# Stick-breaking attention scores on Trainium2: stacking the high and low parts of a head over 128 rows

## The chip, the cores and the metric

The kernel runs on one core of one Trainium2 chip. The metric is the time of the kernel in device microseconds (us). The profile gives one execution in detail: five engines work side by side on their own instruction streams, TensorE (PE, whose weight loads PEld run beside its products), VectorE (DVE), ScalarE (ACT), GpSimd (POOL) and SyncE (SP, which issues most transfers). PSUM, where products are accumulated, has eight banks of 128 partitions by 512 float32 columns.

## The reference

One decoder layer over 512 tokens of width 1024, in three sub-layers: a SwiGLU feed-forward block (inner width 2816), a mixing block, and a second feed-forward block. Each is modulated by vectors computed from a condition, gated, added to the residual and normalised. The mixing block runs two branches side by side. The one that matters here is attention with 16 heads of 64:

```python
z = jnp.einsum('bhqd,bhkd->bhqk', qb, kb).astype(jnp.float32) * scale
mask = s_idx < t_idx
log_keep = jnp.where(mask, jax.nn.log_sigmoid(-z), 0.0)
between = lax.cumsum(log_keep, axis=3, reverse=True) - log_keep
log_w = jax.nn.log_sigmoid(z) + between
w = jnp.where(mask, jnp.exp(log_w), 0.0)
outs.append(jnp.einsum('bhqk,bhkd->bhqd', w.astype(vb.dtype), vb))
```

A weight is thus the sigmoid of its score times the product of (1 - sigmoid) of all later scores in the row. The other branch is a gated linear unit (glu), a causal depthwise convolution of width 31, a normalisation and a swish.

## The kernel before

**Precision.** A product of two float32 matrices is made from parts: each operand is split into a high part, rounded to the matmul format F32R, and a low part, the rest. High times high, high times low and low times high are accumulated in one PSUM bank, so a float32 product takes three matmuls. For a result that is itself an operand of the next product (q, k, v, the attention weights), ACT copies the bank into the high part, and DVE subtracts the high part from the bank into the low part.

**Before the attention.** The first feed-forward block ends with the normalisation of each 128-token tile and its transposition into u2, the input of the mixing block. `dense_group` (L378) then makes the projections of the first pair of heads (q, k, and glu's two halves), four tiles of 128 output channels by 512 tokens, and `run(v_tasks(0))` the first group of v.

**The unit loop (L733).** Attention goes by units. A unit `i` is one head and one tile of 128 query tokens: pair of heads j = i // 8, head hh in the pair, token tile tb, 64 units in all. A tile of q or k holds one pair, head 0 in partitions 0 to 63, head 1 in 64 to 127. An iteration of the loop does, in this order:

- `att_scores(i)` (L623): the scores z of the unit, 128 queries by n = (tb + 1) x 128 keys, from three matmuls whose contraction runs over the 64 rows of the head (L630 to L632). Two sigmoids on ACT (L635, L636) give nb = sigmoid(-z) and be = sigmoid(z), a scan on DVE (L637) the running product of nb, and POOL masks and multiplies (L640, L642).
- `advance`: one or two half tasks from a list `tasks` made beforehand: a projection tile is two halves of 12 matmuls, a group of v (two pairs of heads) four blocks of 24. A planner orders them by due times: q and k of pair j are due two units before the pair begins, and a group of v at the start of the pairs that use it. The other tasks, glu and gates, fill the rest. Weights are fetched three tasks ahead (`AHEAD`).
- `att_values(i - 3)` (L661): weights times v, three matmuls for each of the tb + 1 key tiles into 64 columns (128*64 tiles) of the bank po.
- `att_transpose(i - 2)` (L645): the weights are transposed by PE (pw, L652) and split into wTh (ACT, L655) and wTl (DVE, L656).
- `bg`: on average 3.8 (`CONV_PACE`) pieces of background work, the taps of the depthwise convolution on DVE (L527). A finished glu pair adds 32 pieces to the list.
- in each fourth of the first 32 iterations, one multiplication or addition on POOL over a residual tile (L316).

**Buffers that the change touches.** Projections and v pass through three PSUM banks (tag `ps`). The first half of a glu pair keeps its bank until the second half is evicted (`glu_done`, L566). Scores have two banks (`z`). The parts of q and k (`qh`, `ql`, `kh`, `kl`) have two buffers each, so that pair j + 1 can be written while pair j is read. The parts of v (`vh`, `vl`) are tiles of 4 x 256 columns, one for a group of two pairs, two buffers each. The buffers of a tag are handed on: a new tile is written only after the last reader of the tile that had its place. Waits between engines are worked out from such reads and writes. The order on each engine is made when the program is built; it follows the order of the text, where what an instruction needs is there.

**After the attention** come five rounds of a gate tile and a tile of the attention's output projection, with 14 background pieces each (L830), the normalisation of the convolution, which needs all taps, and the rest of the merge.

Of the kernel before, what the change touches and what calls it, by code (L numbers as in the profile page):

```python
# [7 lines left out]
F32 = mybir.dt.float32  # L8
F32R = mybir.dt.float32r
# [5 lines left out]
P = 128  # L15
S = 512
D = 1024
KC = D // P
NT = S // P
# [3 lines left out]
DH = 64  # L23
# [20 lines left out]
def decoder_block(ctx: ExitStack, tc: tile.TileContext, a: dict, out: bass.AP):  # L44
    nc = tc.nc
# [463 lines left out]
    at_cm, ap_ = open_pool("mixa", "left")  # L509
# [3 lines left out]
    qk = {}  # L513
    vq = {}
# [16 lines left out]
            background.append(lambda i=i: tap(i))  # L531
        background.append(lambda: nc.vector.tensor_add(acc, acc, accs[1]))

    def parts_of(ps, name, bufs):
        hi = ap_.tile([P, S], F32R, tag=name + "h", name=name + "h", bufs=bufs)
        lo = ap_.tile([P, S], F32R, tag=name + "l", name=name + "l", bufs=bufs)
        nc.scalar.copy(hi, ps)
        nc.vector.tensor_sub(lo, ps, hi.bitcast(F32))
        return hi, lo

    def gate_tile(name):
        return gp.tile([P, S], F32, tag="g", name=name, bufs=4)

# [8 lines left out]
    def tile_tasks(src, name, done):  # L552
        st = {}
        return [(lambda: st.update(w=load_added(src)), lambda: half_dense(st, name, 0, done)),
                (None, lambda: half_dense(st, name, 1, done))]

    def set_qk(j, x, ps):
        qk[j, x] = parts_of(ps, x, 2)

    def qk_tasks(j):  # L560
        out_ = []
# [28 lines left out]
    def v_tasks(q):  # L590
        st = {}

        def block(t):
            if t == 0:
                st["h"] = ap_.tile([P, NT, 256], F32R, tag="vh", name="vh", bufs=2)
                st["l"] = ap_.tile([P, NT, 256], F32R, tag="vl", name="vl", bufs=2)
                vq[q] = (st["h"], st["l"])
            if t % 2 == 0:
                st["ps"] = bank("psv")
            ps = st["ps"]  # L600
            o = ps[:, (t % 2) * 256 : (t % 2) * 256 + 256]
            tsl = slice(t * P, (t + 1) * P)
            for k in range(KC):
                wh, wl = st["w"][k // 4]
                cs = slice((k % 4) * 256, (k % 4) * 256 + 256)
                nc.tensor.matmul(o, u2[0][:, k, tsl], wh[:, cs], start=(k == 0), stop=False)
                nc.tensor.matmul(o, u2[0][:, k, tsl], wl[:, cs], start=False, stop=False)
                nc.tensor.matmul(o, u2[1][:, k, tsl], wh[:, cs], start=False, stop=(k == KC - 1))
            if t % 2 == 1:
                dst = st["h"][:, t - 1 : t + 1, :]  # L610
                pv = ps.rearrange("p (t e) -> p t e", t=2)
                nc.scalar.copy(dst, pv)
                nc.vector.tensor_sub(st["l"][:, t - 1 : t + 1, :], pv, dst.bitcast(F32))

        def fetch():
            st["w"] = [load_added(a["w_v"][q, h]) for h in range(2)]

        return [(fetch if t == 0 else None, lambda t=t: block(t)) for t in range(NT)]
# [3 lines left out]

    def att_scores(i):  # L623
        j, hh, tb = i // 8, (i // 4) % 2, i % 4
        (qh, ql), (kh, kl) = qk[j, "q"], qk[j, "k"]
        rs = slice(hh * DH, (hh + 1) * DH)
        n = (tb + 1) * P
        tsl = slice(tb * P, (tb + 1) * P)
        z = bank("z", "z")
        nc.tensor.matmul(z[:, :n], qh[rs, tsl], kh[rs, :n], start=True, stop=False)  # L630
        nc.tensor.matmul(z[:, :n], qh[rs, tsl], kl[rs, :n], start=False, stop=False)
        nc.tensor.matmul(z[:, :n], ql[rs, tsl], kh[rs, :n], start=False, stop=True)  # L632
        nb = ap_.tile([P, S], F32, tag="nb", name="nb", bufs=2)
        be = ap_.tile([P, S], F32, tag="be", name="be", bufs=LAG + 1)
        nc.scalar.activation(nb[:, :n], z[:, :n], AF.Sigmoid, scale=-QSCALE)  # L635
# [24 lines left out]

    def att_values(i):  # L661
        j, hh, tb = i // 8, (i // 4) % 2, i % 4
        vh, vl = vq[j // 2]
        wh, wl = unit.pop(i)
        rs = slice(hh * DH, (hh + 1) * DH)
        vs = slice((j % 2) * P + hh * DH, (j % 2) * P + (hh + 1) * DH)
        tsl = slice(tb * P, (tb + 1) * P)
        if tb == 0:
            heads["po"] = bank("po", "po")
# [320 lines left out]
```

## Time and profile before

| | |
|---|---|
| Time, median of 3 runs | 1331.72 us (1330.6 to 1331.79) |
| The profiled execution: its own time | 1331.39 us |
| Its span (first to last instruction) | 1329.7 us |
| Granted TensorE clock, mean | 0.995 |
| PE busy / PEld busy | 1289.2 us (97%) / 1068.7 us |
| DVE / ACT / POOL busy | 739.4 / 523.0 / 567.8 us |
| Unit loop, first score product to the start of the last gate tile in it | 422.8 to 729.2 us |
| Score products in it | 192, first start 422.8, last 712.0 us |

The times come from runs without a profile; every duration comes from the one profiled execution. Matmuls overlap in their pipeline, so the duration of one says less than the distance from its start to the next start. A wait "x <- y" is idle time of the engine just before x that ended when y did. A line such as L630 is the line of the kernel that issued the instruction; in helpers such as `dense` (L144 to L146) the tile's name tells which projection it is.

### The profile page before, as it was taken

To read this page: it belongs to the slowest core of one execution; us is meant where nothing else is said; L and a number is where in the kernel's file an instruction comes from. 1 tells how busy PE (TensorE), PEld (TensorE's weight loads), DVE (VectorE), ACT (ScalarE), POOL (GpSimd) and SP (SyncE) were. 2 spreads that over 40 slices of the span, in tenths; PEclk is the share of its full clock that TensorE was granted. 3 is DMA by queue.
4 is the path that set the end of the run, shared out by engine and by line. 5 is a ranking of instruction groups with operands and counts; after the bars stand their busy time and mean duration, and the time that the engine had idled before them with its cause. 6 is when DMAs were issued, how large, how long until landed. Compare 5 with 4: busy or idle time off the path is not lost.

```text
span 1329.7 us, 16789 instructions
## 1 busy us (share of the span) xinstructions
PE 1289.2 (97%) x6444; PEld 1068.7 (80%) x6444; DVE 739.4 (56%) x1017; ACT 523.0 (39%) x793; POOL 567.8 (43%) x392
## 2 busy tenths in 40 slices
PE   5899999999999999999999999997999999999997
PEld 4688888888889878878778888885898888888886
DVE  7886920255463959498788865366682000025545
ACT  2233322222256555555555648422452222222220
POOL 3464544644312564533443111142254566564434
PEclk9999999999999999999999999998999999999999
DMA  9668843232328474656466985974283333323321
GB/s 358 216 213 310 299 160 94 97 96 95 95 83 196 103 174 96 140 129 130 110 144 132 237 196 112 294 219 140 68 281 96 96 110 97 114 101 93 102 65 63
DMA packets 57856, 197.88 MB, mean 149 GB/s; under 512 B 6688, under 2 KB 6832, under 8 KB 57776
## 3 DMA queue, kind: packets, MB, share of 16 engines
q1 hardware_dynamic: 47952, 161.15, 36.6%
q0 software_dynamic: 9824, 35.66, 15.7%
q8 instruction: 50, 0.82, 0.2%
q14 instruction: 30, 0.25, 0.1%
HBM read 194.70 MB, written 2.10 MB: 148 GB/s over the span
## 4 chain that ended last, share of the span: by engine, by line
PE 85%; DVE 10%; DMA 2%; ACT 1%; POOL 1%; issue 1%; SPq 0%; DVEq 0%; POOLq 0%; ACTq 0%
PE y L357 19%; DVE ada L189 3%; DVE cacc L527 2%; PE z L630 1%; PE q L144 1%; PE glub L144 1%; PE glua L144 1%; PE pw L652 1%; PE ga L146 1%; PE ga L144 1%; PE ga L145 1%; PE gb L146 1%; PE gb L145 1%; PE gb L144 1%; PE q L145 1%; PE glub L145 1%
## 5 line engine op out<-in xcount | busy, mean ns | idle before, releaser
L114 POOL TENSOR_TENSOR wlo<-raw,whi 128x1024 fp32r<-128x1024 f32 x88 | 223.3, 2543 | 244.4 <-ACT whi L113 240.2
L113 ACT CAST whi<-raw 128x1024 fp32r<-128x1024 f32 x144 | 149.6, 1046 | 275.2 <-issue 50.6
L137 POOL TENSOR_TENSOR raw<-raw,mod_g 128x1024 f32<-128x1024 f32 x52 | 131.4, 2532 | 154.8 <-DMA raw<-in_dn 85.8
L527 DVE SCALAR_TENSOR_TENSOR cacc<-h,cv_w,cacc 128x512 f32<-128x512 f32 x232 | 173.8, 809 | 0.0
L130 ACT CAST whi<-raw 128x1024 fp32r<-128x1024 f32 x68 | 71.3, 1049 | 123.7 <-PE ga L145 19.9
L114 DVE TENSOR_TENSOR wlo<-raw,whi 128x1024 fp32r<-128x1024 f32 x56 | 104.7, 1871 | 23.6 <-ACT whi L113 23.6
L357 PE MATMUL y<-whi,sh 128*128 128x512 f32 x352 | 113.7, 390 | 0.0
L357 PE MATMUL y<-wlo,sh 128*128 128x512 f32 x352 | 113.6, 389 | 0.0
L357 PE MATMUL y<-whi,sl 128*128 128x512 f32 x352 | 113.6, 389 | 0.0
L189 DVE SCALAR_TENSOR_TENSOR ada<-ada,crow 128x512 f32<-128x512 f32 x96 | 92.0, 1007 | 13.5 <-DMA ada<-in_ada_t 8.3
L642 POOL TENSOR_TENSOR be<-be,nb 128x127 f32<-128x127 f32 (+1 forms) x64 | 55.0, 860 | 102.8 <-DVE nb L637 101.4
L422 DVE TENSOR_TENSOR sl<-sF,sh 128x512 fp32r<-128x512 f32 x44 | 45.3, 1031 | 85.4 <-ACT sh L421 85.4
L421 ACT CAST sh<-sF 128x512 fp32r<-128x512 f32 x44 | 27.1, 623 | 143.7 <-PE y L357 132.0
L132 POOL DMA_DIRECT2D wlo<-in_w_in x44 | 38.4, 873 | 92.2 <-ACT wlo L131 88.4
L357 PEld LDWEIGHTS y<-whi,sl 128*128 128x128 f32 x352 | 66.1, 188 | 13.7
L357 PEld LDWEIGHTS y<-wlo,sh 128*128 128x128 f32 x352 | 66.1, 188 | 13.7
L357 PEld LDWEIGHTS y<-whi,sh 128*128 128x128 f32 x352 | 66.1, 188 | 13.6
L131 ACT ACTIVATE wlo<-whi 128x1024 fp32r<-128x1024 f32 x68 | 72.1, 1061 | 0.9
L637 DVE TENSOR_TENSOR_SCAN nb<-nb,future 128x127 f32<-128x127 f32 (+1 forms) x64 | 60.3, 942 | 2.0 <-ACT nb L635 1.8
L640 POOL TENSOR_SCALAR_AFFINE_SELECT be<-be 128x128 f32<-128x128 f32 x64 | 43.4, 678 | 22.6 <-ACT be L636 22.0
L224 DVE SCALAR_TENSOR_TENSOR acc<-ada,silu_c,acc 128x1024 f32<-128x1024 f32 x21 | 43.6, 2078 | 14.4 <-DMA ada<-in_ada_w 14.2
L656 DVE TENSOR_TENSOR wTl<-pw,wTh 128x128 fp32r<-128x128 f32 (+1 forms) x64 | 30.5, 477 | 32.2 <-ACT wTh L655 32.1
(496 smaller groups left out, 3362.4 us busy)
## 6 DMA issues: line engine op xcount, KB each, us to landing
raw<-in_gu SPq DMA_DIRECT2D x80, 512.0 KB, 3.6
raw<-in_w_in SPq DMA_DIRECT2D x48, 512.0 KB, 3.6
raw<-in_dn SPq DMA_DIRECT2D x44, 512.0 KB, 3.5
wlo<-in_w_in POOLq DMA_DIRECT2D x44, 512.0 KB, 6.9
ada<-in_ada_t SPq DMA_DIRECT2D x32, 512.0 KB, 5.1
ada<-in_ada_w SPq DMA_DIRECT2D x24, 512.0 KB, 4.8
ada<-in_ada SPq DMA_DIRECT2D x32, 256.0 KB, 6.0
raw<-in_gu_first SPq DMA_DIRECT2D x8, 512.0 KB, 6.4
```

The lines of the kernel that those rows point to most:

```text
L113: nc.scalar.copy(hi, raw)
L114: lo_eng.tensor_sub(lo, raw, hi.bitcast(F32))
L130: nc.scalar.copy(hi, raw)
L131: nc.scalar.mul(lo, hi.bitcast(F32), -1.0)
L137: nc.gpsimd.tensor_mul(raw, raw, G)
L144: nc.tensor.matmul(ps[:, c0:c1], wh[:, ks], mov(uh, k)[:, c0:c1], start=(k == 0), stop=False)
L145: nc.tensor.matmul(ps[:, c0:c1], wh[:, ks], mov(ul, k)[:, c0:c1], start=False, stop=False)
L189: ins = nc.vector.scalar_tensor_tensor(raw[:, qs], raw[:, qs], 1.0, crow[:, qs], ALU.mult, ALU.mult, accum_out=parts[:, q : q + 1])
L357: nc.tensor.matmul(acc[t][h][:, c0 - h * 512 : c1 - h * 512], st[:, tsl], wt[:, c0:c1], start=(k == 0 and i == 0 and c0 % 512 == 0), stop= ...
L527: ins = nc.vector.scalar_tensor_tensor(o, hv, cv_w[:, j, i : i + 1], o, ALU.mult, ALU.add)
L637: nc.vector.tensor_tensor_scan(nb[:, 1:n][:, ::-1], nb[:, 1:n][:, ::-1], future[:, S - n + 1 : S][:, ::-1], 1.0, ALU.mult, ALU.max)
L642: nc.gpsimd.tensor_mul(be[:, 0 : n - 1], be[:, 0 : n - 1], nb[:, 1:n])
```

## The change

- `att_scores` makes z from two matmuls instead of three, each with a contraction over all 128 partitions. For head hh, `q1` holds the high part of the head's q twice (in the head's own 64 partitions and in the other 64), `k12` the high part of k in the own partitions and the low part in the others, so their product is hi x hi + hi x lo. `q2` holds the low part of q in the own partitions and zeros in the others; its product with `k12` is lo x hi.
- `set_qk` builds these tiles per head. For q, two ACT copies of 64 partitions (own, then other) and one DVE subtraction per head; for k, one ACT copy and one DVE subtraction per head, the subtraction written into the other partitions. The tiles `q0`, `q1`, `k0`, `k1` have two buffers each. The `q2` tiles are four that stay (`qlow`, by parity of j and by head).
- Before the first dense group, the zero halves of the four `qlow` tiles are written: one memset on POOL, four ACT copies of 64 partitions.
- The parts of v are kept by pair of heads, tiles of 4 x 128 columns with three buffers each instead of tiles for two pairs with two buffers. At the first block of a group both pairs' tiles are allocated, and each eviction of a bank (after the second and the fourth block) is two ACT copies and two DVE subtractions of 256 columns instead of one each of 512.

```diff
--- before.py
+++ after.py
@@ -531,13 +531,6 @@
             background.append(lambda i=i: tap(i))
         background.append(lambda: nc.vector.tensor_add(acc, acc, accs[1]))
 
-    def parts_of(ps, name, bufs):
-        hi = ap_.tile([P, S], F32R, tag=name + "h", name=name + "h", bufs=bufs)
-        lo = ap_.tile([P, S], F32R, tag=name + "l", name=name + "l", bufs=bufs)
-        nc.scalar.copy(hi, ps)
-        nc.vector.tensor_sub(lo, ps, hi.bitcast(F32))
-        return hi, lo
-
     def gate_tile(name):
         return gp.tile([P, S], F32, tag="g", name=name, bufs=4)
 
@@ -554,8 +547,32 @@
         return [(lambda: st.update(w=load_added(src)), lambda: half_dense(st, name, 0, done)),
                 (None, lambda: half_dense(st, name, 1, done))]
 
+
+
+    half = [slice(0, DH), slice(DH, P)]
+    qlow = [[ap_.tile([P, S], F32R, **({} if i + hh else {"align_bytes": 256}), name=f"ql{i}{hh}") for hh in range(2)]
+            for i in range(2)]
+    zero = ap_.tile([P, S], F32, tag="nb", name="zero", bufs=2)
+    nc.gpsimd.memset(zero, 0.0)
+    for set_ in qlow:
+        for hh in range(2):
+            nc.scalar.copy(set_[hh][half[1 - hh], :], zero[half[1 - hh], :])
+
     def set_qk(j, x, ps):
-        qk[j, x] = parts_of(ps, x, 2)
+        both = []
+        for hh in range(2):
+            own, other = half[hh], half[1 - hh]
+            t = ap_.tile([P, S], F32R, tag=f"{x}{hh}", name=f"{x}{hh}", bufs=2)
+            nc.scalar.copy(t[own, :], ps[own, :])
+            if x == "q":
+                low = qlow[j % 2][hh]
+                nc.vector.tensor_sub(low[own, :], ps[own, :], t[own, :].bitcast(F32))
+                nc.scalar.copy(t[other, :], ps[own, :])
+                both.append((t, low))
+            else:
+                nc.vector.tensor_sub(t[other, :], ps[own, :], t[own, :].bitcast(F32))
+                both.append(t)
+        qk[j, x] = both
 
     def qk_tasks(j):
         out_ = []
@@ -592,9 +609,8 @@
 
         def block(t):
             if t == 0:
-                st["h"] = ap_.tile([P, NT, 256], F32R, tag="vh", name="vh", bufs=2)
-                st["l"] = ap_.tile([P, NT, 256], F32R, tag="vl", name="vl", bufs=2)
-                vq[q] = (st["h"], st["l"])
+                for j in (2 * q, 2 * q + 1):
+                    vq[j] = [ap_.tile([P, NT, P], F32R, tag="v" + x, name="v" + x, bufs=3) for x in "hl"]
             if t % 2 == 0:
                 st["ps"] = bank("psv")
             ps = st["ps"]
@@ -607,10 +623,12 @@
                 nc.tensor.matmul(o, u2[0][:, k, tsl], wl[:, cs], start=False, stop=False)
                 nc.tensor.matmul(o, u2[1][:, k, tsl], wh[:, cs], start=False, stop=(k == KC - 1))
             if t % 2 == 1:
-                dst = st["h"][:, t - 1 : t + 1, :]
                 pv = ps.rearrange("p (t e) -> p t e", t=2)
-                nc.scalar.copy(dst, pv)
-                nc.vector.tensor_sub(st["l"][:, t - 1 : t + 1, :], pv, dst.bitcast(F32))
+                for j in range(2):
+                    h_, l_ = vq[2 * q + j]
+                    dst, part = h_[:, t - 1 : t + 1, :], pv[:, :, j * P : (j + 1) * P]
+                    nc.scalar.copy(dst, part)
+                    nc.vector.tensor_sub(l_[:, t - 1 : t + 1, :], part, dst.bitcast(F32))
 
         def fetch():
             st["w"] = [load_added(a["w_v"][q, h]) for h in range(2)]
@@ -622,14 +640,12 @@
 
     def att_scores(i):
         j, hh, tb = i // 8, (i // 4) % 2, i % 4
-        (qh, ql), (kh, kl) = qk[j, "q"], qk[j, "k"]
-        rs = slice(hh * DH, (hh + 1) * DH)
+        (q1, q2), k12 = qk[j, "q"][hh], qk[j, "k"][hh]
         n = (tb + 1) * P
         tsl = slice(tb * P, (tb + 1) * P)
         z = bank("z", "z")
-        nc.tensor.matmul(z[:, :n], qh[rs, tsl], kh[rs, :n], start=True, stop=False)
-        nc.tensor.matmul(z[:, :n], qh[rs, tsl], kl[rs, :n], start=False, stop=False)
-        nc.tensor.matmul(z[:, :n], ql[rs, tsl], kh[rs, :n], start=False, stop=True)
+        nc.tensor.matmul(z[:, :n], q1[:, tsl], k12[:, :n], start=True, stop=False)
+        nc.tensor.matmul(z[:, :n], q2[:, tsl], k12[:, :n], start=False, stop=True)
         nb = ap_.tile([P, S], F32, tag="nb", name="nb", bufs=2)
         be = ap_.tile([P, S], F32, tag="be", name="be", bufs=LAG + 1)
         nc.scalar.activation(nb[:, :n], z[:, :n], AF.Sigmoid, scale=-QSCALE)
@@ -660,10 +676,10 @@
 
     def att_values(i):
         j, hh, tb = i // 8, (i // 4) % 2, i % 4
-        vh, vl = vq[j // 2]
+        vh, vl = vq[j]
         wh, wl = unit.pop(i)
         rs = slice(hh * DH, (hh + 1) * DH)
-        vs = slice((j % 2) * P + hh * DH, (j % 2) * P + (hh + 1) * DH)
+        vs = rs
         tsl = slice(tb * P, (tb + 1) * P)
         if tb == 0:
             heads["po"] = bank("po", "po")
```

## The prediction

> **What bounds the kernel now.** I read the page first: the engine totals, then the chain of work that ended last.
>
> ```profile
> PE 1289.2 (97%) x6444; PEld 1068.7 (80%) x6444; DVE 739.4 (56%) x1017; ACT 523.0 (39%) x793; POOL 567.8 (43%) x392
> PE 85%; DVE 10%; DMA 2%; ACT 1%; POOL 1%; issue 1%; SPq 0%; DVEq 0%; POOLq 0%; ACTq 0%
> ```
>
> PE carries the span, so time taken from PE's stream shortens it, as long as nobody else is late there. DVE's 56% is a mean over stages, and the change lies in one: the unit loop, from the first score product to the last gate tile in it (the attention stage). I cut it into seven stretches of iterations of the unit loop. The list of background convolution taps, at 3.8 an iteration, has work in the first, third, fifth and seventh stretch (iterations 0-8, 14-22, 29-44, 48-66) and runs dry in the others (9-13, 23-28, 45-47); this follows from when the loop finishes each glu pair. The view of busy time by stretch:
>
> ```profile
> 422.76:461.21 38.45, 37.09 (x228) 30.11 (x227) 33.70 (x46) 19.73 (x38) 20.11 (x23) 1.00 0.65 140
> 461.21:486.86 25.65, 25.22 (x154) 20.26 (x153) 12.70 (x18) 15.16 (x27) 16.75 (x18) 1.00 0.63 144
> 486.86:526.34 39.48, 39.48 (x242) 31.66 (x241) 36.11 (x51) 21.91 (x43) 18.92 (x25) 1.00 0.63 134
> 526.34:556.59 30.25, 29.09 (x193) 24.41 (x193) 16.96 (x19) 16.04 (x30) 18.94 (x17) 1.00 0.45 105
> 556.59:630.05 73.46, 73.08 (x461) 59.68 (x461) 62.12 (x94) 41.76 (x79) 31.12 (x45) 1.00 0.61 137
> 630.05:643.28 13.23, 13.23 (x77) 10.37 (x77) 11.60 (x18) 7.76 (x15) 6.31 (x10) 1.00 0.60 126
> 643.28:729.16 85.88, 85.88 (x496) 68.58 (x496) 73.69 (x113) 45.63 (x83) 33.34 (x47) 1.00 0.60 128
> ```
>
> Columns: stretch, its length, then busy time of PE, PEld, DVE, ACT and POOL, granted clock, DMA share, GB/s. PE is busy 303 of 306 us. DVE is the runner-up: 85 to 91% in the four tap stretches. The clock is 1.00 throughout.
>
> **What a unit costs on PE.** One unit in order of time, the values of an older unit first; then the weight loads of the first score product and of the next dense product:
>
> ```profile
> 559.76 0.39 PE L146 MATMUL glub<-uh,wlo 128*128 128x512 f32 x1
> 559.98 0.22 PE L675 MATMUL po<-wTh,vh 128*64 128x128 f32 x1
> ...
> 560.46 0.22 PE L677 MATMUL po<-wTh,vl 128*64 128x128 f32 x1
> 560.52 0.62 PE L652 MATMUL pw<-ident,be 128*128 128x128 f32 x4
> 561.07 0.44 PE L630 MATMUL z<-kh,qh 64*128 64x384 f32 x1
> 561.35 0.34 PE L631 MATMUL z<-kl,qh 64*128 64x384 f32 x1
> 561.53 0.33 PE L632 MATMUL z<-kh,ql 64*128 64x384 f32 x1
> 561.79 0.50 PE L144 MATMUL glua<-uh,whi 128*128 128x512 f32 x1
> 562.13 0.40 PE L145 MATMUL glua<-ul,whi 128*128 128x512 f32 x1
> 562.36 0.40 PE L146 MATMUL glua<-uh,wlo 128*128 128x512 f32 x1
> ```
>
> ```profile
> 561.07 0.18 PEld L630 LDWEIGHTS z<-kh,qh 64*128 64x128 f32 x1 [0.17 <-issue]
> 561.79 0.19 PEld L144 LDWEIGHTS glua<-uh,whi 128*128 128x128 f32 x1 [0.25 <-issue]
> ```
>
> Durations overlap, so what counts is start to start. In the dense stream a 512-column product takes 0.23 us (562.13 to 562.36), its weights loaded ahead. The step from dense into the values tile (559.76 to 559.98) is no longer than that. But at both edges of the 64-row score products the weight load stands idle 0.17 and 0.25 us and starts only together with its own product. For comparison, transposes followed by a dense product where all tiles are 128*128:
>
> ```profile
> 803.72 1.04 PE L799 MATMUL ptb<-ident,cn 128*128 128x128 f32 x8
> 804.52 0.48 PE L144 MATMUL ysb<-ph,whi 128*128 128x512 f32 x1
> 804.83 0.40 PE L145 MATMUL ysb<-pl,whi 128*128 128x512 f32 x1
> ```
>
> Eight transposes and one product take 1.11 us: less 0.23, that is 0.11 a transpose and nothing over. In the unit, four transposes and the first score product take 561.35 - 560.52 = 0.83, where 4 x 0.11 + 0.18 = 0.62 would do: 0.21 over. From the last score product to the second dense one are 562.13 - 561.53 = 0.60, where 0.18 + 0.23 = 0.41 would do: 0.19 over. So each unit pays about 0.40 us for entering and leaving the 64-row shape.
>
> **What the change takes off PE.** Two score products replace three; the steps that they take, from the rows (384 columns: 0.18 above):
>
> ```profile
> 552.58 0.27 PE L631 MATMUL z<-kl,qh 64*128 64x128 f32 x1
> 552.69 0.27 PE L632 MATMUL z<-kh,ql 64*128 64x128 f32 x1
> 556.81 0.28 PE L631 MATMUL z<-kl,qh 64*128 64x256 f32 x1
> 556.93 0.27 PE L632 MATMUL z<-kh,ql 64*128 64x256 f32 x1
> 565.94 0.39 PE L631 MATMUL z<-kl,qh 64*128 64x512 f32 x1
> 566.17 0.39 PE L632 MATMUL z<-kh,ql 64*128 64x512 f32 x1
> ```
>
> That is 0.11, 0.12, 0.18 and 0.23 us, 0.64 for four units, 16 x 0.64 = 10.2 us in all. Contracting 128 rows instead of 64 costs nothing per product: 0.23 for 512 columns at either height. The scores now have the 128*128 shape of their neighbours, so the 0.40 goes too, 64 x 0.40 = 25.6. Gross 35.8 us, 0.56 a unit. Bounds for the edge: 0 (it was something else, and stays) and 0.40; I take all of it, since the row of 128*128 neighbours shows no excess.
>
> One rule speaks against the last step. The Trainium skill, TensorEngine Tiling, Key Properties, says that changing the tiling mode drains the TensorE. By that rule the change of shape at the values tile (128*64) drains as well, and if the 0.40 is shared by all four changes of a unit, the sum loses half of it, 12.8 us. The trace agrees at the 64-row edges (0.17 and 0.25 idle) and shows no drain at the 64-column tile (0.22 from dense to values).
>
> **What it adds.** Rows for evictions, scan and weighting:
>
> ```profile
> L679 ACT COPY yF<-po 64x512 f32<-64x512 f32 x16 | 9.2, 577 | 20.5 <-PE po L677 20.4
> L538 DVE TENSOR_TENSOR ql<-q,qh 128x512 fp32r<-128x512 f32 x7 | 4.8, 688 | 9.9 <-ACT qh L537 9.7
> L656 DVE TENSOR_TENSOR wTl<-pw,wTh 128x256 fp32r<-128x256 f32 x16 | 6.5, 406 | 2.3 <-ACT wTh L655 2.3
> L637 DVE TENSOR_TENSOR_SCAN nb<-nb,future 128x511 f32<-128x511 f32 x16 | 21.5, 1342 | 0.9 <-ACT nb L635 0.9
> L642 POOL TENSOR_TENSOR be<-be,nb 128x511 f32<-128x511 f32 x16 | 17.5, 1092 | 26.9 <-DVE nb L637 26.5
> ```
>
> ACT takes 0.58 us for 64x512, and moves it to other partitions for the second head, so half the partitions is not half the time. Each q tile now takes four ACT copies for one and two DVE subtractions for one; each k tile two and two. In the stage (seven pairs) that is 7 x 4 x 0.58 = 16 us on ACT, whose busy time is 168 of 306: hidden by its idle time. On DVE it is 14 x 0.69 = 9.6 us, if a subtraction on 64 partitions takes as long as one on 128. Splitting six v evictions adds 6 x (2 x 0.41 - 0.69) = 0.8.
>
> This is where the gain is cut. Per stretch I take off 0.56 x units (9, 5, 9, 6, 16, 3, 16) from the length, add to DVE 1.4 for each pair of q and k and 0.13 for each v eviction, and let the later end count: 33.4 against 35.2 (DVE); 22.9 against 14.2 (PE); 34.4 against 37.5 (DVE); 26.9 against 18.6 (PE); 64.5 against 65.2 (DVE); 11.6 against 11.6; 76.9 against 75.1 (PE). The sum of the later ones is 276.2, so 306.4 - 276.2 = 30.2 is left of 35.8; DVE takes 5.6. A backlog of one iteration would be made up in the dry stretches: at best this loss is 0.
>
> Three smaller terms. The evictions, first. The PSUM bank of a projection is freed by the subtraction, and in two places PE waits for that now (the view of waits, then the chain at one of them):
>
> ```profile
> PEld k L144 <- DVE ql L538: 1.6, 2, 0.8
> ```
>
> ```profile
> 547.69 0.59 ACT qh L537
> 548.31 0.70 DVE ql L538
> 549.05 0.50 PE k L144
> ```
>
> There glu's two banks are held, and the rest passes through the third. The eviction takes 0.59 + 0.70 = 1.3 us; with four copies, the second subtraction ends some 1.0 later. Two places: 2.0 us (bounds 0 and seven times 1.0).
>
> The v tiles, second. Before there were two buffers of two pairs; now there are three of one pair, filled two at a time. The second pair's buffer is free only when the pair three back has had its last values: iteration 10 for the group evicted at 7, iteration 26 for the one evicted at 23, and the bank stays held meanwhile. Around 23 only one bank is free (glu again), so v, q and k stand behind it, and PE has only units to do. Least: 0, if units and the open glu half fill the time. Most: one unit's chain, scores 0.72, ACT 0.58, scan 1.34, POOL 1.09, transposes 0.55, ACT 0.58, DVE 0.69, values 0.72: 6.3 us. I take 1.0 at iteration 10, where only the last values are missing, 2.5 at 23, none for the third group (banks free): 3.5.
>
> The start, third. One memset and four 64x512 copies (4 x 0.58 = 2.3 us on ACT) make the zero halves ahead of the first dense group. ACT has room before that:
>
> ```profile
> 373.84 1.86 ACT L291 ACTIVATE uf<-ps_tr,B,A 128x128 f32<-128x128 f32 x5 [10.27 <-PE ps_tr L287]
> ```
>
> If the memory is free by then the cost is 0; if not, up to 2.3, plus 1.5 for three more copies of the first q ahead of the next weights' low part. I take 1.5 of 0 to 3.8. The products after the stage are untouched; POOL loses nothing but the memset.
>
> **Sum.** 35.8 - 5.6 - 2.0 - 3.5 - 1.5 = 23.2 us. The profiled execution took 1331.4 (span 1329.7), 0.3 below the median 1331.7. So 1331.4 - 23.2 = 1308.2; on the median's scale that is 1308.5.
>
> **Rivals.** (1) DVE's backlog is absorbed and the waits are filled: gain near the gross 35.8, 1296 to 1300. For it: stretches two and four leave DVE half idle. Against: waits for banks exist already. Chance 0.18. (2) DVE sets the pace for good: its idle gaps, mostly waits for ACT's casts, don't close, so the tap stretches give back twice the 5.6, and both waits cost their upper ends (7 and 6.3): 35.8 - 11.2 - 7 - 6.3 - 1.5 = 9.8, 1322. For it: 85 to 91% busy. Against: three stretches of PE slack. Chance 0.12. (3) Half of the 0.40 belongs to the values tile, whose shape stays different from its neighbours', and remains: 64 x 0.20 = 12.8, gross 23.0; DVE then takes 1.4, the other terms 7.0: gain 14.6, 1317. Against: the step of 0.22 from dense to values. Chance 0.06. It is what the Trainium skill's page TensorEngine Tiling (Key Properties) would give. (4) The edge stays whole, the change does not do what it could: 10.2 gross, none lost to DVE, 7.0 to the waits: gain 3.2, 1328. Chance 0.05. (5) Slower: the v buffers. If each of the six evictions in the stage stops PE for a whole unit's chain, because dense work and values stand behind the eviction in the engines' order, 6 x 6.3 = 38 replaces the 3.5: 35.8 - 5.6 - 2.0 - 1.5 - 38 = -11, 1343. It decides from 26.7 / 6 = 4.4 us per eviction on. Against: at 10 only values are missing, and for the third group banks are free. Chance 0.06.
>
> **Numbers.** The forecast case, 1301 to 1315, has 0.53. Range 1297 to 1321: it takes in rivals 3 and most of 1, about half of 2. A difference of 0.2% (2.7 us) is about what a measurement of this kernel tells from none. Faster 0.91, same 0.03 (from rival 4, and mishaps between), slower 0.06.
>
> **What would show it.** Right: in the attention stage 128 score products of 128*128; the first one's weight load starting before its product, four transposes and a 384-column product in 0.62; units nearer 4.0 than 4.6 us apart; DVE above 95% in the tap stretches; new PE waits named after the v evictions near iterations 10 and 23, and after q's second subtraction. Wrong: the weight loads still idle 0.17 at the scores; units apart as before with DVE full; gaps of PE of several us at each v group; or a subtraction on 64 partitions with shifted output that takes far more than 0.69.

## The result, and the profile after

The changed kernel takes 1347.27 us (median of 4 runs, 1346.76 to 1349.19), the kernel before 1331.39 (1330.6 to 1331.79): a ratio of 1.0122, 95% interval 1.0108 to 1.0136. It is 16 us slower; 23 us faster had been forecast. The profiled span grew from 1329.7 to 1347.2 us, by 17.5.

The changed kernel's page, its busy times, its rows of 40 slices and the head of its chain:

```profile
span 1347.2 us, 16719 instructions
PE 1273.9 (95%) x6380; PEld 1067.6 (79%) x6380; DVE 754.8 (56%) x1041; ACT 543.4 (40%) x837; POOL 570.7 (42%) x393
...
PE   5899999999999889789899999997999999999997
...
PE 72%; DVE 20%; ACT 3%; issue 2%; DMA 1%; POOL 1%; SPq 0%; DVEq 0%; POOLq 0%; ACTq 0%
```

The row of PE in the kernel before:

```profile
PE   5899999999999999999999999997999999999997
```

PE's busy time fell by 15.3 us (1289.2 before). Its idle time, span less busy, rose from 40.5 to 73.3, by 32.8; the difference is the 17.5. The new dips of the PE row lie in slices 14 to 20, in the attention stage, where the row of before has a 9 throughout. DVE's share of the chain doubled from 10 to 20%.

One unit in order of time, from the changed kernel's timeline:

```profile
463.27 0.52 PE L668 MATMUL pw<-ident,be 128*128 128x128 f32 x3
463.54 0.36 PE L647 MATMUL z<-k,q 128*128 128x256 f32 x1
463.75 0.28 PE L648 MATMUL z<-k,ql 128*128 128x256 f32 x1
463.86 0.29 PE L622 MATMUL psv<-whi,uh 128*128 128x256 f32 x1
463.99 0.28 PE L623 MATMUL psv<-wlo,uh 128*128 128x256 f32 x1
```

The scores are 128*128, the dense product follows the second one after 0.11 us, and three transposes and the first score product take 0.48 where 3 x 0.11 + 0.13 = 0.46 would do (0.13 is the step of a dense product of 256 columns, 463.86 to 463.99). So the edge is gone, as forecast. What came is in the view of waits, PE's between 400 and 735 us:

```profile
PE po L692 <- DVE wTl L672: 10.1, 12, 3.2
PE po L691 <- ACT wTh L671: 9.8, 5, 4.2
PE pw L668 <- POOL be L658: 6.5, 4, 3.5
PE k L144 <- DVE vl L631: 2.5, 1, 2.5
PE q L144 <- DVE vl L631: 2.2, 2, 1.3
PE k L144 <- ACT sg L585: 1.8, 1, 1.8
PE q L144 <- ACT uh L294: 1.4, 2, 1.2
```

Total us, times, longest. In the kernel before the same view has four rows, 3.4 us in all; the largest:

```profile
PE po L676 <- DVE wTl L656: 1.8, 3, 1.4
```

Most of the waits now are the values' (`po`), for the two parts of the weights that the same unit's transposes gave. How the longest comes about, in the timelines of DVE, ACT and PE from 595 us on:

```profile
595.08 2.84 DVE L527 SCALAR_TENSOR_TENSOR cacc<-h,cv_w,cacc 128x512 f32<-128x512 f32 x4
597.84 0.94 DVE L653 TENSOR_TENSOR_SCAN nb<-nb,future 128x383 f32<-128x383 f32 x1
598.71 0.66 DVE L569 TENSOR_TENSOR ql<-q,q 64x512 fp32r<-64x512 f32 x1
600.60 0.69 DVE L569 TENSOR_TENSOR ql<-q,q 64x512 fp32r<-64x512 f32 x1 [1.24 <-ACT q L566]
...
596.35 0.58 ACT L566 CAST q<-q 64x512 fp32r<-64x512 f32 x1
596.83 1.06 ACT L131 ACTIVATE wlo<-whi 128x1024 fp32r<-128x1024 f32 x1
599.40 0.58 ACT L570 CAST q<-q 64x512 fp32r<-64x512 f32 x1 [1.51 <-DVE ql L569]
599.99 0.58 ACT L566 CAST q<-q 64x512 fp32r<-64x512 f32 x1
600.59 0.58 ACT L695 COPY yF<-po 64x512 f32<-64x512 f32 x1
601.20 0.27 ACT L671 CAST wTh<-pw 128x128 fp32r<-128x128 f32 x1
...
597.03 0.28 PE L648 MATMUL z<-k,ql 128*128 128x128 f32 x1
601.51 0.37 PE L691 MATMUL po<-wTh,vh 128*64 128x128 f32 x1 [4.21 <-ACT wTh L671]
```

ACT makes the first copy of a q tile at 596.35. DVE's subtraction from it stands behind four taps and a scan and starts at 598.71. ACT's next copy from that bank waits for the subtraction, and behind it in ACT's queue stand a third copy, a copy of `po`, and only then the `wTh` of 0.27 us that PE has needed since 597.3. ACT has idle time here (busy 4.44 of the 10 us in the first window below), DVE has little (9.37), and each queue holds something short behind something long. The whole eviction, from the first copy to the end of the second subtraction (600.60 + 0.69), takes 4.9 us.

Such a gap costs twice. Two windows of the changed kernel (columns as in the prediction's table), then q's products after another gap:

```profile
590.00:600.00 10.00, 6.78 (x50) 5.57 (x48) 9.37 (x15) 4.44 (x8) 3.52 (x6) 0.98 0.42 98
600.00:610.00 10.00, 8.49 (x31) 6.77 (x32) 8.33 (x12) 3.80 (x10) 3.46 (x5) 0.68 0.35 55
```

```profile
476.19 0.55 PE L668 MATMUL pw<-ident,be 128*128 128x128 f32 x3 [3.53 <-POOL be L658]
477.59 0.79 PE L144 MATMUL q<-uh,whi 128*128 128x512 f32 x1 [0.86 <-DVE vl L631]
478.18 0.63 PE L145 MATMUL q<-ul,whi 128*128 128x512 f32 x1
478.61 0.63 PE L146 MATMUL q<-uh,wlo 128*128 128x512 f32 x1
...
483.30 0.48 PE L145 MATMUL q<-ul,whi 128*128 128x512 f32 x1
483.62 0.39 PE L146 MATMUL q<-uh,wlo 128*128 128x512 f32 x1
483.85 0.39 PE L144 MATMUL q<-uh,whi 128*128 128x512 f32 x1
```

After a gap of 3.5 us a dense product steps 0.43 us (478.18 to 478.61) instead of 0.23 (483.62 to 483.85), for 6 us. Over the whole run the granted clock is 0.985 against 0.995; one per cent of 1347 is some 13 us by my estimate, and an upper one, since PE also has waits while the clock is low. The Trainium skill, TensorE: Matmul & The Clock Gate, "What's actually happening", says that the clock falls to half after an idle window of about 3.4 us and comes back after as long a busy one; the trace agrees, with 0.43 against 0.23 after a gap of 3.5 us, though the full rate came back after 6. A gap of 3.17 us, before 449.57, was enough as well (products of 256 columns then step 0.21 us, where 0.12 is the full rate), and there the full rate was back after 3.2.

### The profile page after: what moved, and what is told of

It reads as the page before. It is cut to its first block, busy times and chain, and to the rows that moved or that the text cites. A ratio compares the mean times of both kernels' runs of the same rounds, so it can differ in the third digit from the quotient of the medians.

```text
span 1347.2 us, 16719 instructions
## 1 busy us (share of the span) xinstructions
PE 1273.9 (95%) x6380; PEld 1067.6 (79%) x6380; DVE 754.8 (56%) x1041; ACT 543.4 (40%) x837; POOL 570.7 (42%) x393
## 4 chain that ended last, share of the span: by engine, by line
PE 72%; DVE 20%; ACT 3%; issue 2%; DMA 1%; POOL 1%; SPq 0%; DVEq 0%; POOLq 0%; ACTq 0%
PE y L357 19%; DVE cacc L527 8%; DVE ada L189 3%; DVE nb L653 3%; DVE wTl L672 1%; PE gb L146 1%; PE gb L145 1%; PE gb L144 1%; PE ga L144 1%; PE ysb L144 1%; PE ysb L145 1%; PE ga L145 1%; PE ysb L146 1%; PE ga L146 1%; PE ycv L146 1%
## 5 line engine op out<-in xcount | busy, mean ns | idle before, releaser
L527 DVE SCALAR_TENSOR_TENSOR cacc<-h,cv_w,cacc 128x512 f32<-128x512 f32 x232 | 175.6, 815 | 0.1
L130 ACT CAST whi<-raw 128x1024 fp32r<-128x1024 f32 x68 | 71.3, 1048 | 124.5 <-PE ga L145 19.9
L357 PEld LDWEIGHTS y<-wlo,sh 128*128 128x128 f32 x352 | 66.1, 188 | 13.7
L357 PEld LDWEIGHTS y<-whi,sl 128*128 128x128 f32 x352 | 66.1, 188 | 13.7
L357 PEld LDWEIGHTS y<-whi,sh 128*128 128x128 f32 x352 | 66.1, 188 | 13.7
L656 POOL TENSOR_SCALAR_AFFINE_SELECT be<-be 128x128 f32<-128x128 f32 x64 | 43.6, 682 | 25.3 <-ACT be L652 25.2
L464 PE MATMUL first<-uh,whi 128*128 128x512 f32 x64 | 27.0, 422 | 18.8 <-ACT whi L113 18.8
```

Source lines behind the costliest of these rows:

```text
L130: nc.scalar.copy(hi, raw)
L357: nc.tensor.matmul(acc[t][h][:, c0 - h * 512 : c1 - h * 512], st[:, tsl], wt[:, c0:c1], start=(k == 0 and i == 0 and c0 % 512 == 0), stop= ...
L527: ins = nc.vector.scalar_tensor_tensor(o, hv, cv_w[:, j, i : i + 1], o, ALU.mult, ALU.add)
```

## Experiments

Each ratio is to the kernel before on the same chip (its median there 1330.4 to 1331.0). The edits are shown shortened. In the expectations V is the theory that the three v buffers cost the time, A that ACT and DVE alternate on a bank, and the others are named where they come.

**Parts of the change alone.** In the first run the scores are as changed and v as before; to make room for that, the tiles `k0` have one buffer and the low queries of head 0 one tile; the second and third run change v alone, with three and four buffers.

```
e1   vq[q] = (vh, vl)  # v, its eviction and its reads as before
     k0: bufs=1; ql00 serves for ql10 too
e2   kernel before, with vq[j] = [... [P, NT, P] ..., bufs=3] and the two-part eviction
e3   the same, bufs=4
```

> The changed scores, q and k as in the change, but the v tiles as before (two buffers of two pairs). For the room that this needs, k's tile of head 0 has one buffer instead of two and both parities share head 0's low tile. Theory V (the three v buffers of one pair are what costs: an eviction waits for the pair three back, PE runs out of dense work, and the clock is halved after the gap): the gain of the scores comes out, 1303 to 1316 us, PE waits at the values under 5 us in all, granted clock in the loop above 0.98 everywhere. Rival E (the longer evictions of q and k on ACT and DVE cost, wherever v lies): 1335 to 1348, waits for wTh and wTl as in the changed kernel (20 us), clock drops remain.

> The kernel before with only the v tiles changed to three buffers of one pair; scores, q and k as before. Theory V: slower by what the buffers cost, 20 to 40 us: 1351 to 1371, with units bunched at iterations 9 to 13, 24 to 30 and 36 to 37 as in the changed kernel, and clock drops. Rival E: within 4 us of before, 1328 to 1336.

> As the kernel before, with v tiles of one pair, but four buffers, as much room as before. Theory V: no wait for a buffer, so 1329 to 1334 (the split evictions add 0.8 us on DVE). Rival S (splitting the eviction costs, not the number of buffers): as slow as with three buffers. Rival E says the same as V here.

Measured: 1339.2 us, ratio 1.0064 (1.0047 to 1.0081); 1339.5, 1.0066 (1.0049 to 1.0083); 1331.8, 1.0006 (0.9996 to 1.0016). Splitting the v evictions is free within the interval. Three buffers instead of four cost some 8 us in a kernel with the old scores: less than theory V said, more than rival E. The first run made waits of its own by its single tiles (`z` for `ql` 7.6 us), so it says only that the loss isn't v's alone.

Why three buffers cost that much shows in the order in which PE's instructions were laid out (name, number of instructions; units 7 to 13):

```
before  psv24 po9 pw4  z3 q12 po12 pw1  z3 q12 po3 pw2  z3 k12 po6 pw3  z3 k12 glub12 po9 pw4
after   psv24 po9 pw4  z2 pw1  z2 po1  z1 po11 pw2  z1 pw3 q24 po3 k12 po6  z2 k12 glub12 po9 pw4
```

The group of v evicted around iteration 7 needs the tile of pair 0, which values read until iteration 10. In the text's order these values stand behind the dense work that needs the evicted banks, so that order can't be kept: units 8 to 12 are laid out close together and the dense work comes in a lump behind. In the changed kernel's trace `z` starts at 463.54, 469.52, 469.99 and 471.23, and no dense work lies between the last three. With nothing to fill them the chains of these units show: that is the gap of 3.53 us above.

**v later, copies first.** The first kernel is the change with a v group planned behind the next pair's q and k; the second has all of an eviction's copies ahead of its subtractions; the third both.

```
e4  -    urgent += [(8 * j + 8, f) for f in v_tasks(j // 2 + 1)]   # j odd
    +    urgent += [(8 * j, f) for f in v_tasks(j // 2)]           # j even
e5  +    for hh in range(2): nc.scalar.copy(ts[hh][half[hh], :], ps[half[hh], :])
    +    if x == "q": for hh in range(2): nc.scalar.copy(ts[hh][half[1 - hh], :], ps[half[hh], :])
    +    for hh in range(2): nc.vector.tensor_sub(...)             # v likewise
```

> The changed kernel, with each group of v put behind the q and k of the next pair in the planner's list instead of ahead of them (due two units later than those, at the start of the pair that uses it), so that it is evicted at iterations 10 to 13, 26 to 29 and 42 to 45, when the pair three back has had its last values. Three buffers as in the change. Theory V: most of the loss goes, 1305 to 1320, gaps of PE at v under 2 us each. Rival E: 1340 to 1350.

> The whole change with one thing reordered: in each eviction of q, k and v all ACT copies out of the bank come first and all DVE subtractions after them, the same instructions otherwise. In the change they alternate, and the program makes each further ACT copy of the bank wait for the DVE subtraction before it (the trace shows ACT idle 1.95 us before the second k copy, released by DVE), which stands behind convolution taps; behind the copy wait the casts of the weights and the sigmoids. Theory A (this alternation stops ACT's queue): PE's waits for wTh and wTl fall below 12 us, clock drops to 3 or 4, time 1320 to 1334. Rival D (the added DVE work itself, whatever its order): waits and time as in the change, 1340 to 1349.

> As the run before, and the groups of v planned behind the next pair's q and k, so that their buffers are free. Theory A: both losses gone but the start (3 us) and DVE's limit: 1310 to 1324. Rival D: 1335 to 1344, as with v later alone (1342).

Measured: 1342.0, 1.0087 (1.0071 to 1.0104); 1348.1, 1.0130 (1.0109 to 1.0151); 1345.0, 1.0112 (1.0096 to 1.0127). v later returns 5 us, the order of the copies by itself nothing: theories V and A as the sole cause fall. With copies first and v later, PE waits 28.4 us for `wTl` alone:

```profile
PE po L689 <- DVE wTl L669: 28.4, 21, 4.0
```

The same view has 1.5 us for `wTh`. With v later alone it has 19.4 for `wTl` and 12.4 for `wTh`: the delay has moved from ACT's queue into DVE's.

**The evictions alone.** The kernel before with its q and k evictions in two halves, alternating and copies first; no other part of the change.

```
e7  +  for rows in (slice(0, DH), slice(DH, P)):
    +      nc.scalar.copy(hi[rows, :], ps[rows, :])
    +      nc.vector.tensor_sub(lo[rows, :], ps[rows, :], hi[rows, :].bitcast(F32))
e8     the two copies, then the two subtractions
```

> The kernel before, scores and v untouched, only q's and k's evictions cut into two halves of 64 partitions that alternate: ACT copy, DVE subtraction, ACT copy, DVE subtraction. It adds 14 subtractions on DVE (9.6 us) and 14 copies on ACT in the loop. Theory A: slower by 8 to 20 us, 1339 to 1351, with waits for wTh. Rival D: slower too, and by as much as the run after this one.

> As the run before, the same four instructions for each tile, but both ACT copies first, then both subtractions. Theory A: most of the cost of the alternation is gone, at most 5 us over before: 1330 to 1336. Rival D: as slow as the alternating one, within 2 us.

Measured: 1343.5, 1.0107 (1.0085 to 1.0128); 1345.5, 1.0118 (1.0101 to 1.0135). That was the surprise: 14 copies of 0.58 and 14 subtractions of 0.69 us in the loop, 18 us in all on two engines with idle time, cost 13 to 15 us over the kernel before on that chip (1330.5). The two orders differ by 2 us, as rival D said. In the second kernel's timeline the chain of one unit can be followed: `wTl` of three blocks starts at 449.33, in the kernel before at 446.28, 3.05 later, 0.8 of it from the start of the stage, and PE waits 3.4 us for it where it waited 1.4.

**VectorE's load, and four mends.** The taps halved in both kernels (i % 4 >= 2 left out, 1.9 an iteration); the change with mends; the control of its pace.

```
e9, e10  +  if i % 4 < 2: background.append(...)        CONV_PACE = 1.9
e11         v later as above; CONV_PACE = 3.5
         +  nc.tensor.matmul = lambda *x, **kw: tc.keep_in_program_order(matmul(*x, **kw))   # in the loop
         +  nc.gpsimd.tensor_copy(low[half[1 - hh], :], zero[half[1 - hh], :])               # behind v_tasks(0)
e12         kernel before, CONV_PACE = 3.5
```

> The whole change, and of the 31 taps of each convolution 15 are left out (those with i % 4 >= 2), handed to VectorE at 1.9 instead of 3.8 in an iteration. So 8 x 15 = 120 taps of about 0.74 us are missing, some 60 of them beside the units. Theory D (in the loop VectorE is as full as TensorE, an iteration of the kernel before has 3.8 x 0.74 of taps + 0.90 scan + 0.48 wTl + 0.2 to 0.3 of evictions = 4.5 us beside 289 / 63 = 4.6 us between first score products, so what TensorE saves can't be used): with the taps halved the gain of the scores shows, 1305 to 1318 us, at least 12 below the kernel before with the same taps left out. Theory O (the order in which TensorE's instructions were laid out around the v groups, units ahead of the dense work, and the half clock after the gaps that it makes): that order is the same in this kernel, so the loss stays and it is within 5 us of the kernel before with half the taps. Theory E (ScalarE's added copies and the wait of its copies for VectorE): little change either, 1335 to 1345.

> The control: the kernel before with the same 15 taps of each convolution left out, 1.9 in an iteration. Its TensorE has hardly a wait in the loop (3.4 us in all), so theory D, O and E all say 1322 to 1331: a few us for the waits in the loop and for taps that end late after it.

> The whole change with four mends: v groups planned behind q and k of the next pair; TensorE's instructions in the loop kept in the order of the text; the zero halves written by GpSimd behind the first v group instead of by ScalarE ahead of the first dense group; taps 3.5 in an iteration instead of 3.8. Nothing is left out. Theory D: an iteration has 3.5 x 0.74 + 1.4 + 0.4 = 4.4 us of VectorE, so the loop still goes at about 4.4 us and ends some 10 us earlier than in the change with v later (1342); the start gives 3 us back, 20 more taps behind the loop cost up to 7: 1328 to 1336. Theory O: with the order put right the loss is gone, 1310 to 1322. Theory E: 1338 to 1344, as the evictions are the same.

> The control for the pace: the kernel before with 3.5 taps in an iteration instead of 3.8. Theory D: the waits in the loop shrink by 1 to 3 us, 20 taps more behind the loop cost 0 to 7: 1329 to 1337. Theory O and E: 1330 to 1336.

Measured: 1328.8, 0.9983 (0.9970 to 0.9995); 1327.0, 0.9974 (0.9961 to 0.9987); 1340.6, 1.0078 (1.0058 to 1.0098); 1330.2, 1.0000 (0.9991 to 1.0010). Halved taps take 18 us off the change and 3 off the kernel before (1330.4 on that chip). That is none of the theories whole: D wanted the change 12 us under its control; O's number, within 5 us of the control, came true (1.8), but not its reason that the loss stays, as 16 us over the kernel before became 2; E wanted 1335 at least. The run with mends is in E's range. The mends are good for 7 us in all, the first score product at 422.7 as before (425.8 in the change), so the 3 us of the start are among them. What was left shows in ACT's waits with the mends: among the seven largest groups are two for DVE, where the seven largest of the kernel before are all for PE:

```profile
ACT vh L625 <- DVE vl L626: 14.6, 5, 7.2
ACT q L565 <- DVE ql L564: 10.1, 5, 3.1
```

**Evictions taken away, and a unit of slack.** In the first, both heads of a pair read head 0's tiles and head 1 isn't evicted. The second is the mended change with half the taps, 3.8 / 2 an iteration. In the third the values stand one unit later; the fourth is its control.

```
e13  -  for hh in range(2):        +  for hh in (0,):   ...  qk[j, x] = both * 2
e14     e9 and e11 (v later, order, zero halves)
e15  -  if i > LAG: att_values(i - LAG - 1)
     +  if i > LAG + 1: att_values(i - LAG - 2)         # wTh, wTl: bufs=3; q0, k0: bufs=1
e16     kernel before, values a unit later, order of the text
```

> The whole change, but of q and k only head 0 of each pair is evicted, and both heads of the pair read its tiles: 2 copies and 1 subtraction for a q, 1 and 1 for a k, against 4 and 2, 2 and 2 in the whole change and 1 and 1 in the kernel before. TensorE's work is that of the change; head 1 of each pair is left out. If the added evictions cost what they cost in the kernel before by themselves (12 to 14 us), whether as work or as delay: 1330 to 1336. If they cost nothing beside the v groups' order: 1343 to 1348.

> v groups later, TensorE in the order of the text, zero halves by GpSimd behind the first v group, and half the taps left out as in the run of the whole change with half the taps (1328.8; the kernel before with half the taps 1327.0). If VectorE's load and the order are separate losses that add: 1328.8 - 8 - 3 = 1314 to 1321. If what is left is delay in the unit's chain by the evictions, v later gives little more: 1322 to 1328. If VectorE's load was all that was left after the order: 1300 to 1308.

> Nothing left out. v groups later, TensorE in the order of the text, zero halves by GpSimd; and the values of a unit stand one unit later (three buffers for wTh and wTl; one for the tiles of head 0 of q and k, which pays for them). Theory of the delay (a q eviction puts 2.3 us of copies on ScalarE and 1.4 on VectorE ahead of the next wTh and wTl, and the values have less than a unit, 4 us, to spare): the waits of po for wTh and wTl, 27 us in the run with the four mends, fall to a few, 1308 to 1320, faster than before. Theory of the load (VectorE has 3.8 x 0.74 + 1.4 + 0.4 = 4.6 us in an iteration): the waits turn up elsewhere and the time stays at 1335 to 1342.

> The control: the kernel before with the values of a unit one unit later and TensorE in the loop in the order of the text. It has 3.4 us of waits in the loop, so both theories say 1326 to 1332.

Measured: 1332.1, 1.0005 (0.9996 to 1.0014); 1314.2, 0.9871 (0.9855 to 0.9887); 1338.4, 1.0056 (1.0039 to 1.0073); 1327.8, 0.9970 (0.9960 to 0.9981). Without the added evictions (one added copy of each q is left) the change is as fast as the kernel before, so they cost 15 us in it too. Load and order do more than add: mends that are worth 7 us with all taps (the slower pace among them) are worth 14.6 with half of them (1328.8 to 1314.2). The third run's time is in the range of the theory of the load, but it is inconclusive, for its single tiles stalled the queue that they were to relieve (PE's waits there):

```profile
PE psv L738 <- ACT q L565: 13.8, 2, 7.6
PE po L738 <- ACT yF L690: 9.2, 3, 8.4
PE k L738 <- ACT q L565: 5.0, 1, 5.0
```

**All mends.** Values a unit later need no third buffer after all: `wTh` of unit i + 2 is written behind the values that read unit i. So every tile keeps two. The second kernel rids itself of the 64-row products in another way: three products, q tiles per head with zero halves, k as before.

```
e17  e11, values a unit later (bufs=2), copies first
e18  the same, with
  +  nc.scalar.copy(hi[half[hh], :], ps[half[hh], :])   # for each head; subtractions behind
  +  matmul(z, qh, kh); matmul(z, qh, kl); matmul(z, ql, kh)
```

> Nothing left out. The four mends (v groups later, TensorE in the order of the text, zero halves by GpSimd behind the first v group, taps 3.5 in an iteration; 1340.6 with these alone), values a unit later with two buffers for each tile, and in each eviction all of ScalarE's copies ahead of VectorE's subtractions, so that no copy waits for a subtraction. If the loss is delay in queues without slack: TensorE's waits in the loop, 31 us with the four mends, fall under 8 and the clock goes back towards 0.995, 1308 to 1322. If it is VectorE's load (3.5 x 0.74 + 1.4 + 0.4 = 4.4 us in an iteration, 63 x 4.4 = 277 us against 289 between the first and the last score product before, and taps behind): VectorE is over 90% busy from 425 to 700 us and the time is 1328 to 1338.

> The same mends on another way to be rid of the 64-row products: three products over 128 rows as qh.kh + qh.kl + ql.kh, where each head's queries lie in tiles whose other 64 rows are zero and the keys stay pair tiles. An eviction of q is 2 copies and 2 subtractions, of k 1 and 1 as in the kernel before: a third of the added ScalarE copies and half of the added VectorE subtractions of q and k; the 0.40 us for entering and leaving the 64-row shape is gone as in the change, the third product is back (10 us). Delay: 1308 to 1322, about as the run beside it. Load: 4.8 us of VectorE less than that run, 1324 to 1333.

Measured: 1311.3 us, 0.9851 (0.9830 to 0.9872), and 1313.5, 0.9862 (0.9835 to 0.9889). Both beat the two kernels. The first computes everything, with all the evictions and taps of the change, and is 36 us faster than it (by its ratio too: 0.9851 against 1.0122). PE's waits of that kernel between 400 and 735 us (its products in the loop bear the line of the helper that keeps their order):

```profile
PE po L735 <- DVE wTl L664: 8.4, 6, 3.0
PE k L735 <- DVE ql L566: 3.5, 1, 3.5
PE po L735 <- ACT yF L687: 1.4, 2, 0.8
PE pw L736 <- POOL be L650: 0.4, 1, 0.4
```

The stretch from 425 to 729 us, in the kernel before, in the changed one and in that with all mends:

```profile
425.00:729.00 304.00, 300.67 (x1831) 243.05 (x1830) 245.78 (x354) 165.60 (x307) 144.34 (x179) 1.00 0.60 131
```

```profile
425.00:729.00 304.00, 270.60 (x1684) 230.51 (x1684) 241.25 (x350) 175.58 (x334) 141.20 (x174) 0.95 0.57 125
```

```profile
425.00:729.00 304.00, 290.20 (x1847) 250.28 (x1846) 273.79 (x393) 198.56 (x362) 146.52 (x182) 0.98 0.64 146
```

DVE goes from 241 to 274 of 304 us, 90%, and still PE is busy 290 at a clock of 0.98. So over the whole loop DVE wasn't full in the change, and load as the bound of the loop falls: the time that it asked for, 1328 to 1338, was missed, though its other sign came (DVE is busy 248.2 of the 275 us from 425 to 700). Delay in queues without slack is what the runs show in the main. Its expectation was met in the time, not in the waits (13.7 us where under 8 was said), and the clock came back to 0.991. Load has a share in the delay: for stretches DVE is full in the change, 24.9 of the 25 us from 450 to 475, and what it must do then is late. What share of the 29 us between the four mends and all of them belongs to the values' place and what to the copies' order was not parted; copies first with v later, but the values in their old place, gained nothing. The values a unit later gain 3 us in the kernel before, so some 16 us of the 20 under it are the change's own. The two last kernels can't be told apart, though the second has a quarter of the added copies and half of the added subtractions of q and k: the dropped product is worth nothing measurable next to its evictions, and the edges carry the gain.

## Why the prediction was wrong

**Gross gain, 35.8: right.** The unit shows the edge gone, and in the kernel with all mends PE's busy time is 1260.4 us, 28.8 under before, at a mean clock of 0.991:

```profile
PE 1260.4 (96%) x6380; PEld 1060.9 (81%) x6380; DVE 759.0 (58%) x1041; ACT 541.6 (41%) x833; POOL 570.2 (44%) x397
```

With an estimate of 5 us for the clock (0.004 x 1309) that makes 34. Rivals 3 (gross 23.0) and 4 (10.2) are excluded by this. The loss that rival 3 left at the 128*64 tile, by the Trainium skill's page TensorEngine Tiling (Key Properties), isn't there: in the changed kernel's timeline the step from dense into the values is 0.12 us (462.79 to 462.91), as between two dense products of 256 columns, and out of them 0.06 (463.21 to 463.27), as between two of the values.

**VectorE, -5.6: the step that failed.** It compared sums of busy time by stretch and let the later end count. That prices an added eviction as work. What it cost was its place: its copies and subtractions stand in two in-order queues ahead of the `wTh` and `wTl` that the values need within a unit, and its later copies wait for its first subtraction. The 16 us of copies on ACT it put at nothing, as hidden by idle time; PE's waits for `wTh`, 9.8 us, are for ACT. The evictions cost 15 us in the change (1347.3 to 1332.1) and 13 to 15 in the kernel before, where 5.6 and, for the bank, 2.0 were reckoned. The prediction priced waits only where a bank was late for dense work. That term, 2.0, takes a q's eviction to last 1.0 us longer than the 1.3 of before; the one shown above lasts 4.9. PE's view has no row for q's subtractions all the same: dense work waits 4.7 us for those of v (`vl`) and 1.8 for glu's bank (`sg`). The values, whose waits are 19.9 us, were never asked what they wait for. That a backlog would be made up in the dry stretches fails, as I read it, for the same reason: a wait of PE isn't given back. (The sixth stretch wasn't dry: DVE is busy 11.60 of its 13.23 us, with taps until 638.7. The sum of the later ends isn't touched by that.)

**v buffers, -3.5: mis-sized.** They cost 8 us alone and 5 in the change. Rival 5 had the mechanism (dense work and values behind the eviction in the engines' order), and the prediction named iterations 10 and 23, but the rival multiplied the wait by six; it came near the measured time with 1343 by luck, for a reason that carries 5 to 8 of the 52 us between the gross gain and the result.

**Start, -1.5: 3.0**, inside its bounds. The four zero copies were held by the memset and stood ahead of `uf` in ACT's queue; behind the first v group on POOL they leave the first score product where it was (422.7).

**Clock: not priced.** The prediction said that it is 1.00 throughout and left it there. The longest gap that it allowed for, 6.3 us, is longer than the one of 3.5 after which the clock was half.

The terms don't add up one by one. From 34 gross the v buffers, the evictions and the start take about 26; to end 16 slower, another 24 must go, and no run that undoes one part of the change returns them. Two shares can be named but not added up: the clock (the 13 us estimated above, which the waits bring with them) and DVE's load (halved taps return 18). I read the rest as the same delay: a unit is 0.56 us shorter on PE, so the chain through ACT, DVE and ACT that just fitted in 4.6 us no longer fits. The run with slack and all work in agrees with it; it wasn't shown alone, so this part of the cause stays open. Rival 2, DVE as the pace, had the engine right and the mechanism in part: the wait is for DVE's and ACT's order as much as for their work.

## What to carry to other kernels

When an engine gets faster, ask of each thing it waits for how much slack there is between making and using, before asking how busy its maker is: ACT, busy 58% of the stretch (175.6 of 304 us), still let PE wait 4.2 us for a copy of 0.27 us that stood in its queue behind an eviction in four pieces. Price added copies by what stands behind them in their queue. Give the chain slack first (here, among the mends, the values one unit later, at no memory), then take the gain.

## What the runs showed of the hardware

Two engines that read one bank in turns hand each other their delays: in the changed kernel a copy `k` on ACT waited 4.29 us for DVE's subtraction of the other half, which stood behind four taps that took 5.55 us (four with no POOL instruction beside them, at 622.41, take 2.73):

```profile
442.33 5.55 DVE L527 SCALAR_TENSOR_TENSOR cacc<-h,cv_w,cacc 128x512 f32<-128x512 f32 x4
447.80 0.41 DVE L653 TENSOR_TENSOR_SCAN nb<-nb,future 128x127 f32<-128x127 f32 x1
448.24 0.68 DVE L573 TENSOR_TENSOR k<-k,k 64x512 fp32r<-64x512 f32 x1
...
448.95 0.58 ACT L566 CAST k<-k 64x512 fp32r<-64x512 f32 x1 [4.29 <-DVE k L573]
...
443.16 2.84 POOL L316 TENSOR_TENSOR n<-n,raw 128x1024 f32<-128x1024 f32 x1
```

The taps are 2.82 us longer, as much as the POOL instruction beside them takes. The Trainium skill, SBUF — State Buffer, "Who interferes with whom", says that a VectorE instruction with two inputs in SBUF and a GpSimd instruction that reads SBUF exclude each other; the trace agrees, with 2.84 us of POOL and 2.82 us more of taps. Not every POOL instruction costs the taps time: beside a mask of 0.75 us (L656, 591.35) four take 2.76. Half the partitions are not half the time on DVE either: a subtraction of 64x512 takes 0.69 us on the mean (`k`, L573), of 128x512 0.69 (`ql` in the kernel before).
